# A third seven-product pair in two up panels, and both pairs in both wide down panels of the first part

## The chip, the cores and the metric

The kernel runs on one core of one Trainium2 chip. The metric is the device time of one execution in microseconds (us), the median over the timed runs. One further execution was recorded by the hardware profiler; every duration below comes from it unless it is called a run.

## What is computed

A decoder trunk of two layers over 256 tokens of width 2048, in float32. Layer 0 mixes tokens with gated linear attention, layer 1 with forgetting attention, and both cross-attend into 256 memory tokens. Behind each mixer stands the channel mixer, which is where the change lies:

```python
def causal_dwconv(u, w, b):
    up = jnp.pad(u, ((0, 0), (CONV_WIDTH - 1, 0), (0, 0)))
    return w[0] * up[:, 0:s_] + w[1] * up[:, 1:s_ + 1] + w[2] * up[:, 2:s_ + 2] + b

def conv_ffn(h, w_up, conv_w, conv_b, w_down):
    u = causal_dwconv(h @ w_up, conv_w, conv_b)
    a, val = split_cols(u, [FFN_HIDDEN, FFN_HIDDEN])
    return (jax.nn.silu(a) * val) @ w_down

for i in range(DEPTH):            # DEPTH = 2
    ...
    h = rmsnorm(x, norm_ffn[i])
    x = x + conv_ffn(h, ffn_w_up[i], ffn_conv_w[i], ffn_conv_b[i], ffn_w_down[i])
```

`w_up` is 2048 x 11264 and `w_down` 5632 x 2048, so the two mixers hold most of the matrix work.

## The kernel before, in words

**Numbers in two parts.** Every float32 operand x is split into hi (x rounded to the matmul format, a copy by ScalarE, ACT) and lo (x - hi, a subtraction by VectorE, DVE). One product is then three matmuls: hi by hi, lo by hi, hi by lo. Each weight is loaded raw from HBM in a unit of 128 x 1024 numbers (512 KB), cast by ACT (L257) and subtracted by DVE (L258) before TensorE (PE) can use it. Raw, hi and lo units lie in rings (`class Ring`, L193). In the channel mixer the hi and lo rings have five slots and one guest, and the raw ring five slots and three guests. A slot comes free when the matmuls that read it are done.

**Panels.** The channel mixer (`ffn`, L1419) is a list of panels. An up panel multiplies all 16 chunks of 128 inputs by 1024 columns of `w_up`; there are eleven per layer, and I call them up0 to up10 (`j` = 0, 4, ..., 40 in the code, so the sixth is up5 with `j` = 20 and the ninth up8 with `j` = 32). The hidden width is worked off in three parts (`PARTS`, of 16, 12 and 16 chunks). A wide down panel multiplies the chunks of a part by 1024 output columns. The first part has two of them, d0f0 and d0f2 (`f` = 0 and 2), the second d1f0 and d1f2. The order is up0 to up4, d0f0, d0f2, up5 to up7, d1f0, d1f2, up8 to up10, and then the last part. Every panel runs in each layer.

**Steps of a panel.** `pair_steps` (L409) works a panel off in places, one weight unit to a place. A single unit is a 2 x 2 block of products (two token blocks by two column halves), that is four products or 12 matmuls with 512 columns. Two neighbouring units k and k + 1 make a 2 x 2 by 2 x 2 block product with eight products; if sums of the activation blocks are at hand, they are done with seven (Winograd's form of Strassen's method), 21 matmuls instead of 24. Such a pair, which I call a seven, takes two places. It needs sums of the weight blocks too: four subtractions by DVE (L462 to L465), and four splits (L405 by ACT, L406 by DVE, one of 512 columns and three of 1024) where two singles need two. The dictionary `sums` says which units are paired, and `ahead` at which place.

**Accumulators.** A panel sums into eight accumulators, which are all the banks of PSUM. Seven-only ones (p1, p5, p7, p6) are written by sevens alone, the others (p2, p4, p3, x) by singles as well. After the last seven of a panel `early` (L1373 or L1526) reads the first four; after the last unit, always the single 15 (or 11), `late` (L1385, L1537) reads the other four. `flip` swaps the two sets of banks from panel to panel: the next panel's singles write first into the banks that `early` has read, and its sevens into those that `late` has read. All these reads are DVE instructions, beside one or two ACT copies. In a down panel `early` is eight DVE instructions, four of which add into x (L523).

**Activation sums.** `input_sums(k)` (L1471) makes the sums of the inputs h[k], h[k + 1] for the up panels: two additions of 128 x 256 (L1475), and in `token_sums` (L497) four of 128 x 128 (L501 to L504), a cast by ACT and a subtraction of 128 x 512 by DVE (L713). They are kept in `up_sums` for all panels of a layer: units 6, 7 for every up panel, and units 11, 12 for the panels in `MORE_IN`. For the down panels `gated` (L1458) makes the sums of the hidden chunks when these become known, in two rooms called dsum0 and dsum1; chunks 4, 5 and 10, 11 of the first part have them.

**Work between the steps.** What an up panel yields is scaled, transposed between the partitions by DVE and DMA, put through the convolution (`tap_of` on ACT, `add_tap` on DVE at L1450), silu and product, and split (`gated`, L553 and L554). It is emitted in small pieces between the steps of the following panels: `tick` (L1505) is called once for each place, and hands out pieces by a credit of 1.45 (1.7 beside the panels in `MORE_IN`); the two places of a seven get none. A panel's yield costs 20.4 of such credit. The yield of up4 is put off by 21 places (`PUT_OFF`), so that it falls into d0f2 and up5.

**Order on the engines.** The program is emitted step by step; a planner then fixes each engine's order from estimated times, and gives the weight splits an advance of 300 instructions (`high_priority`). On the chip each engine works its list off in that fixed order.

Of the kernel before, what the change touches and what calls it, by code (L numbers as in the profile page):

```python
# [34 lines left out]
SEVEN_UP = (6,)  # L35
SEVEN_DOWN = {4: 0, 10: 1, 20: 0, 34: 1}
SEVEN_MORE = 11
# [3 lines left out]
RAW_GUESTS = 3  # L41
PUT_OFF = {16: 21}
FIRST_DOWN = (10,)
UP_AHEAD = {8: 1, 40: 1}


LEVELS = (64, 16, 4)
# [105 lines left out]
def _trunk(ctx: ExitStack, tc: tile.TileContext, xt, xtok, memt, wp, wgu, gns, gfin, cnv, par, msk, out):  # L153
# [252 lines left out]
            lows.append(V.tensor_tensor(lo[:, :n], src, hi[:, :n].bitcast(F32), ALU.subtract))  # L406
        return hi, lo

    def pair_steps(units, src, sums, flip, pool, early, late, ahead=0):  # L409

        bank = {}
        fast, slow = ("p1", "p5", "p7", "p6"), ("p2", "p3", "p4", "x")
# [7 lines left out]
        plan = []  # L420
        at = 0
        while at < n:
            if at + ahead in sums:
                plan.append(at + ahead)
                at += 2
            else:
                plan.append(single.pop(0))
                at += 1
# [939 lines left out]
                    steps[f](u)  # L1368


    def down_pair(l, p, f, src, sums, flip, pool, temps, then=None):

        def early(bank):  # L1373
            t0, t1 = temps()
            S.activation(t0, bank["p1"], AF.Copy)
            add_to(f)(0, t0)
            V.tensor_tensor(t0, bank["p6"], t0, ALU.add)
            V.tensor_tensor(t1, bank["p7"], t0, ALU.add)
            add_to(f)(1, t1)
            add_to(f + 1)(1, t1)  # L1380
            add_to(f + 1)(1, bank["p5"])
            V.tensor_tensor(t0, bank["p5"], t0, ALU.add)
            add_to(f + 1)(0, t0)

        def late(b, h, a):  # L1385
            held_back = then is not None and h and not b and then.rooms is not None
            with tc.issue_after(then.turned[-1].ins) if held_back else nullcontext():
                add_to(f + h)(b, a)
            if then is not None:
                then(f + h, b)  # L1390

        return pair_steps(where["down", l, p, f], src, sums, flip, pool, early, late)

    def add_out(key, src, then=None, spare=None, last=None, first=0, hooks=None, late=1):

# [23 lines left out]
    def ffn(l, nx, h, m, more, ys, zs, landing, then, pool, temps, last=None, spare=None):  # L1419
        with tc.tile_pool(name=f"ffn{l}", bufs=1) as fp:  # L1420
            def held(name, i):
                return pool.tile([P, 2, 4, P], F32R, name=name, tag=f"{name}{i}")
# [48 lines left out]
            def input_sums(k):  # L1471

                r = temps(3).rearrange("p (s t) -> p s t", s=2)
                for s in range(2):
                    V.tensor_tensor(r[:, s, :], h[k + s][:, 0, :].bitcast(F32), h[k + s][:, 1, :].bitcast(F32), ALU.add)  # L1475
                token_sums(r, up_sums[k])
# [42 lines left out]
            def up_pair(j):  # L1519

                count[2] += 1
                second = j // 4 in MORE_IN
                turns = [turn(j + 2 * h_, PUT_OFF.get(j) or (7 if not h_ and j // 4 + 1 in MORE_IN else 8)) for h_ in range(2)]
                u = {}

                def early(bank):  # L1526
                    u.update({(b, h_): temps(2 * b + h_) for b in range(2) for h_ in range(2)})
                    S.activation(u[0, 1], bank["p1"], AF.Copy)
                    S.activation(u[0, 0], bank["p1"], AF.Copy, scale=scale(0))
                    V.tensor_tensor(u[0, 1], bank["p6"], u[0, 1], ALU.add)  # L1530
                    V.tensor_tensor(u[1, 0], bank["p7"], u[0, 1], ALU.add)
                    V.tensor_tensor(u[0, 1], bank["p5"], u[0, 1], ALU.add)
                    V.tensor_tensor(u[1, 1], bank["p5"], u[1, 0], ALU.add)
                    for b, h_ in ((0, 1), (1, 0), (1, 1)):
                        S.activation(u[b, h_], u[b, h_], AF.Copy, scale=scale(b))

                def late(b, h_, a):  # L1537
                    with tc.issue_after(turned_last[0].ins) if h_ and not b else nullcontext():
                        V.scalar_tensor_tensor(u[b, h_], a, scale(b), u[b, h_], ALU.mult, ALU.add)
                    turns[h_](b, u[b, h_])  # L1540

                return pair_steps(where["up", l, j], h, {k: up_sums[k] for k in (*SEVEN_UP, SEVEN_MORE)[: 1 + second]},
                                  count[2] % 2, pool, early, late, UP_AHEAD.get(j, 2 * second))

            def first(k):
                {2: lambda: nx.land(landing[0]), 3: nx.take, 8: nx.col,
# [5 lines left out]
            def drive(steps, share=1.45):  # L1552
                for k in steps:
                    tick(share if k >= 0 else 0.0)

            def drive_up(j):
                drive(up_pair(j), 1.7 if j // 4 in MORE_IN else 1.45)

            for k in SEVEN_UP:
                input_sums(k)  # L1560
# [3 lines left out]
            for p, (lo, hi) in enumerate(PARTS[:-1]):  # L1564
                while done < hi + 4:
                    drive_up(done)
                    done += 4
                src = [m[c % RING] for c in range(lo, hi)]
                for f in (0, 2):
                    count[2] += 1  # L1570
                    drive(down_pair(l, p, f, src, {c - lo: t for c, t in sums.items() if (c in FIRST_DOWN) == (f == 0)}, count[2] % 2, pool,
                                    lambda: (temps(0), temps(1))))
                sums.clear()
            lo, hi = PARTS[-1]
            while done < hi:
# [90 lines left out]
    with tc.tile_pool(name="stash", bufs=1) as st:  # L1666
# [4 lines left out]
        with tc.tile_pool(name="turn1", bufs=1) as tp:  # L1671
# [4 lines left out]
            def temps(i):  # L1676
                return fixed[i] if i < 2 else tp.tile([P, 512], F32, name="temp", tag=f"temp{i}")
# [149 lines left out]
```

## Time and profile before

| | |
|---|---|
| median of 3 runs | 2205.3 us (2204.51 to 2207.61) |
| the profiled execution, its own time | 2206.67 us |
| its span, first to last instruction | 2204.9 us |
| busy: POOL | 137.3 us (6%) |
| mean granted TensorE clock | 0.999 |

The span is the profiled execution without what lies around it (1.77 us). A busy share is an average over the whole span; the engines overlap. In a row of a group, the numbers are the engine's busy time, the mean duration of one instruction in ns, and the engine's idle time just before these instructions with what ended it. In a row of a timeline they are start and duration in us. In a row of windows they are the stretch, its length, each engine's busy time with its number of instructions, the granted clock, the DMA share and GB/s.

### The profile page before, as it was taken

The numbers are of one execution on the slowest core, as the hardware profiler recorded it, in microseconds if no ns is written. First come the engines' busy times: TensorE is split into PE (matmuls) and PEld (weight loads), VectorE is DVE, ScalarE is ACT, GpSimd is POOL, SyncE is SP. The second block draws the span as 40 slices with busy tenths as digits, with TensorE's granted clock in tenths as the row PEclk, the third lists the DMA queues.
The fourth block names the chain that finished last, engine by engine and source line by source line (L and its number), as shares of the span: only waits on it lengthen the run. The fifth ranks groups of instructions, "written<-read, shape, count | busy, mean of one in ns | idle before, by whom it ended". The sixth has DMA issues, their size and how long they took to land.

```text
span 2204.9 us, 30083 instructions
## 1 busy us (share of the span) xinstructions
PE 2192.4 (99%) x10285; PEld 1845.2 (84%) x10285; DVE 1836.0 (83%) x2731; ACT 1437.9 (65%) x2282; POOL 137.3 (6%) x257
## 2 busy tenths in 40 slices
PE   9999999999999999999999999999999999999998
PEld 7888888888888888888888998887888888888886
DVE  7768976679998889888987669668999888988996
ACT  6655655556785668657765555555878567765884
POOL 0000000001110010001010000000100001101100
PEclk9999999999999999999999999999999999999999
DMA  9767666777777677767777767676777657766773
GB/s 365 258 222 221 191 212 224 254 234 258 246 259 231 197 225 252 232 205 244 251 241 238 226 201 246 225 242 229 255 263 245 218 197 249 240 230 205 238 273 108
DMA packets 166289, 515.40 MB, mean 234 GB/s; under 512 B 20780, under 2 KB 42552, under 8 KB 166136
## 3 DMA queue, kind: packets, MB, share of 16 engines
q1 hardware_dynamic: 149064, 460.99, 63.4%
q0 software_dynamic: 16496, 51.71, 7.4%
q8 instruction: 80, 1.31, 0.2%
q10 hardware_dynamic: 576, 0.79, 0.1%
q14 instruction: 73, 0.60, 0.1%
HBM read 469.62 MB, written 43.79 MB: 233 GB/s over the span
## 4 chain that ended last, share of the span: by engine, by line
PE 98%; DMA 1%; DVE 0%; ACT 0%; SPq 0%; issue 0%; DVEq 0%; ACTq 0%
PE acc L435 30%; PE acc L362 26%; PE ps_s L435 15%; PE ps_o L435 8%; PE ps_t L435 7%; PE acc L288 3%; PE acc L333 3%; PE ps_s L362 2%; PE acc L392 2%; PE acc L286 1%; DMA raw<-wp 1%; PE ps_s L1060 0%; PE ps_o L726 0%; DMA far<-blk 0%; PE ps_s L726 0%; PE ps_s L1333 0%
## 5 line engine op out<-in xcount | busy, mean ns | idle before, releaser
L258 DVE TENSOR_TENSOR wlo<-raw,whi 128x1024 fp32r<-128x1024 f32 (+2 forms) x613 | 732.1, 1202 | 221.3 <-ACT whi L257 205.5
L257 ACT ACTIVATE whi<-raw 128x1024 fp32r<-128x1024 f32 (+2 forms) x613 | 636.6, 1044 | 368.0 <-PE acc L362 138.2
L362 PE MATMUL acc<-whi,B 128*128 128x512 f32 (+3 forms) x1248 | 290.8, 369 | 0.0
L362 PEld LDWEIGHTS acc<-whi,B 128*128 128x128 f32 x1248 | 226.8, 188 | 28.1
L405 ACT ACTIVATE whi<-raw 128x1024 fp32r<-128x1024 f32 (+1 forms) x154 | 146.6, 952 | 121.4 <-PE ps_t L435 32.5
L406 DVE TENSOR_TENSOR wlo<-raw,whi 128x1024 fp32r<-128x1024 f32 (+1 forms) x154 | 167.4, 1089 | 17.9 <-ACT whi L405 12.8
L435 PE MATMUL acc<-whi,mix 128*128 128x512 f32 x666 | 171.2, 389 | 1.5 <-ACT whi L257 1.5
L435 PE MATMUL acc<-whi,B 128*128 128x512 f32 x650 | 170.9, 389 | 0.0
L362 PE MATMUL acc<-wlo,B 128*128 128x512 f32 (+3 forms) x624 | 159.1, 369 | 0.0
L435 PEld LDWEIGHTS acc<-whi,mix 128*128 128x128 f32 x666 | 124.9, 188 | 27.8 <-ACT whi L257 1.9
L435 PEld LDWEIGHTS acc<-whi,B 128*128 128x128 f32 x650 | 122.0, 188 | 25.4
L1443 ACT ACTIVATE tap<-fvt,cw 128x256 f32<-128x256 f32 x264 | 123.9, 532 | 8.2 <-DMA fvt<-far 7.1
L1443 ACT ACTIVATE tap<-yzu,cw 128x256 f32<-128x256 f32 x264 | 123.8, 531 | 7.5 <-DMA yzu<-far 6.2
L362 PEld LDWEIGHTS acc<-wlo,B 128*128 128x128 f32 x624 | 114.2, 188 | 14.6
L1450 DVE TENSOR_TENSOR tap<-tap,tap 128x1024 f32<-128x1024 f32 x88 | 107.3, 1219 | 0.1
L435 PE MATMUL acc<-wlo,B 128*128 128x512 f32 x325 | 96.2, 389 | 0.0
L435 PE MATMUL acc<-wlo,mix 128*128 128x512 f32 x333 | 95.0, 389 | 0.0
L435 PE MATMUL ps_s<-whi,mix 128*128 128x512 f32 x332 | 92.6, 389 | 0.0
L435 PE MATMUL ps_s<-whi,B 128*128 128x512 f32 x282 | 79.3, 389 | 0.0
L435 PEld LDWEIGHTS acc<-wlo,mix 128*128 128x128 f32 x333 | 62.5, 188 | 13.0
L435 PEld LDWEIGHTS ps_s<-whi,mix 128*128 128x128 f32 x332 | 62.3, 188 | 12.9
L435 PEld LDWEIGHTS acc<-wlo,B 128*128 128x128 f32 x325 | 61.0, 188 | 12.7
(545 smaller groups left out, 4295.7 us busy)
## 6 DMA issues: line engine op xcount, KB each, us to landing
raw<-wp SPq DMA_DIRECT2D x741, 512.0 KB, 4.5
fvt<-far POOLq DMA_DIRECT2D x100, 128.0 KB, 4.8
raw<-wp SPq DMA_DIRECT2D x32, 384.0 KB, 3.6
far<-yu POOLq DMA_DIRECT2D x22, 512.0 KB, 3.4
far<-yzu POOLq DMA_DIRECT2D x22, 512.0 KB, 3.2
yzu<-far POOLq DMA_DIRECT2D x88, 128.0 KB, 4.7
raw<-wp SPq DMA_DIRECT2D x24, 388.0 KB, 3.6
x<-xtok SPq DMA_DIRECT2D x8, 512.0 KB, 7.6
```

The lines of the kernel that those rows point to most:

```text
L257: casts.append(S.activation(hi[:, s], raw[:, s], AF.Copy))
L258: lows.append(V.tensor_tensor(lo[:, s], raw[:, s], hi[:, s].bitcast(F32), ALU.subtract))
L286: mm = TE.matmul(acc[p][c][:, :T], w[:, s], both[:, 0, :], start=False, stop=end and j == 3)
L288: mm = TE.matmul(acc[p][c], w[:, s], both, start=u == j == 0, stop=end and j == 3)
L333: mm = TE.matmul(acc[b][:, :n], src[kcs[j] - base][:, part, b * P : (b + 1) * P], w, start=u == 0 and low == part == j == 0, stop=u == end ...
L362: mm = TE.matmul(acc[b][:, :n], src[kc - base][:, part, b * P : (b + 1) * P], ready[low][:, j * room : j * room + n], start=i == low == pa ...
L392: mm = TE.matmul(acc[b][:, :n], src[kc - base][:, part, b * P : (b + 1) * P], w, start=i == low == part == j == 0, stop=i == end and low = ...
L405: casts.append(S.activation(hi[:, :n], src, AF.Copy))
L406: lows.append(V.tensor_tensor(lo[:, :n], src, hi[:, :n].bitcast(F32), ALU.subtract))
L435: r = TE.matmul(bank[name], x, w, start=name not in begun, stop=last)
L1443: S.activation(by_run(taps[i][:, s, c, i:]), zs[slot][:, :, 2 * c + s], AF.Copy if i else AF.Identity, bias=0.0 if i else w[3], scale=w[2 ...
L1450: V.tensor_tensor(taps[0], taps[0], taps[n][:, :, :, :T], ALU.add)
```

## The change

Up panels get a table of places instead of `ahead`: the key is the place, the value the first unit of the pair.

```diff
-UP_AHEAD = {8: 1, 40: 1}
+UP_STEPS = ({6: 6}, {4: 6, 9: 11}, {1: 6, 5: 11, 10: 2}, {5: 6, 10: 11})
+THIRD, THIRD_IN = 2, (5, 8)
+LATER_IN = (2, 10)
...
-    def pair_steps(units, src, sums, flip, pool, early, late, ahead=0):
+    def pair_steps(units, src, sums, flip, pool, early, late, at_step):
...
-            if at + ahead in sums:
-                plan.append(at + ahead)
+            if at in at_step:
+                plan.append(at_step[at])
...
+                at_step = UP_STEPS[second + (j // 4 in THIRD_IN) + 2 * (j // 4 in LATER_IN)]
...
             def drive_up(j):
-                drive(up_pair(j), 1.7 if j // 4 in MORE_IN else 1.45)
+                share = 1.7 if j // 4 in MORE_IN else 1.45
+                if j // 4 == THIRD_IN[0]:
+                    up_sums[THIRD] = held("dsum", 1)
+                steps = up_pair(j)
+                if j // 4 == THIRD_IN[0]:
+                    for _ in range(4):
+                        tick(share if next(steps) >= 0 else 0.0)
+                    input_sums(THIRD)
+                drive(steps, share)
...
-                    drive(down_pair(l, p, f, src, {c - lo: t for c, t in sums.items() if (c in FIRST_DOWN) == (f == 0)}, count[2] % 2, pool,
-                                    lambda: (temps(0), temps(1))))
+                    steps = down_pair(l, p, f, src, {c - lo: t for c, t in sums.items() if not p or (c in FIRST_DOWN) == (f == 0)}, count[2] % 2, pool,
+                                      lambda: (temps(0), temps(1)), at_step=None if p else {5: 4, 10: 10})
+                    drive(steps)
```

Read out panel by panel: up0 to up4, up6, up7, up9 and up10 keep their pairs and places. up5 and up8 had pairs 6 and 11 at places 4 and 9; they get pair 6 at place 1, pair 11 at place 5 and a new pair 2 at place 10. d0f0 had pair 10 at place 10, and d0f2 pair 4 at place 4; both get pair 4 at place 5 and pair 10 at place 10. The sums for the new pair 2 are made once per layer, in up5 behind four places, in the room dsum1 that d0f2 has just read. The panels of the second and third part's down keep theirs.

More of the change, by code (lines that the diff above doesn't have):

```diff
@@ L1368, in fox, with down_pair @@
                     steps[f](u)
[L1371 removed]
+    def down_pair(l, p, f, src, sums, flip, pool, temps, then=None, at_step=None):
         def early(bank):
@@ L1390, in late @@
                 then(f + h, b)
-        return pair_steps(where["down", l, p, f], src, sums, flip, pool, early, late)
+        return pair_steps(where["down", l, p, f], src, sums, flip, pool, early, late, at_step or {k: k for k in sums})
     def add_out(key, src, then=None, spare=None, last=None, first=0, hooks=None, late=1):
@@ L1540, in late @@
                     turns[h_](b, u[b, h_])
-                return pair_steps(where["up", l, j], h, {k: up_sums[k] for k in (*SEVEN_UP, SEVEN_MORE)[: 1 + second]},
-                                  count[2] % 2, pool, early, late, UP_AHEAD.get(j, 2 * second))
+                at_step = UP_STEPS[second + (j // 4 in THIRD_IN) + 2 * (j // 4 in LATER_IN)]
+                return pair_steps(where["up", l, j], h, {k: up_sums[k] for k in at_step.values()}, count[2] % 2, pool, early, late, at_step)
             def first(k):
```

## The prediction

> **What bounds the kernel now.** I read the page first, from the busy shares to the chain that ended last.
>
> ```profile
> span 2204.9 us, 30083 instructions
> ...
> PE 2192.4 (99%) x10285; PEld 1845.2 (84%) x10285; DVE 1836.0 (83%) x2731; ACT 1437.9 (65%) x2282; POOL 137.3 (6%) x257
> ...
> PE 98%; DMA 1%; DVE 0%; ACT 0%; SPq 0%; issue 0%; DVEq 0%; ACTq 0%
> ...
> L257 ACT ACTIVATE whi<-raw 128x1024 fp32r<-128x1024 f32 (+2 forms) x613 | 636.6, 1044 | 368.0 <-PE acc L362 138.2
> L405 ACT ACTIVATE whi<-raw 128x1024 fp32r<-128x1024 f32 (+1 forms) x154 | 146.6, 952 | 121.4 <-PE ps_t L435 32.5
> L406 DVE TENSOR_TENSOR wlo<-raw,whi 128x1024 fp32r<-128x1024 f32 (+1 forms) x154 | 167.4, 1089 | 17.9 <-ACT whi L405 12.8
> L435 PE MATMUL acc<-whi,mix 128*128 128x512 f32 x666 | 171.2, 389 | 1.5 <-ACT whi L257 1.5
> L1450 DVE TENSOR_TENSOR tap<-tap,tap 128x1024 f32<-128x1024 f32 x88 | 107.3, 1219 | 0.1
> ```
>
> PE is busy 99% and carries 98% of the chain. The channel mixer's matmuls (L435) waited 1.5 us in this group, for an ACT cast. ACT, in contrast, waits for PE: the rings are full and the splits run as far ahead as the slots allow. So time goes where matmuls go, as long as DVE keeps up. Next I asked how full the panels are that the change touches, with the view of windows. The first three stretches are d0f0, d0f2 and up5 of layer 0, then up7, d1f2, up8; the last two are up5 and up8 of layer 1.
>
> ```profile
> core 0: us, PE busy (x) PEld busy (x) DVE busy (x) ACT busy (x) POOL busy (x), PEclk, DMA share, GB/s
> 669.26:712.11 42.85, 42.85 (x191) 35.48 (x190) 37.46 (x48) 22.01 (x28) 5.49 (x10) 1.00 0.74 239
> 712.11:754.94 42.83, 42.83 (x190) 35.47 (x189) 36.91 (x43) 30.28 (x47) 0.00 (x0) 1.00 0.61 203
> 754.94:797.10 42.16, 42.16 (x187) 34.91 (x186) 34.02 (x40) 22.87 (x25) 0.00 (x0) 1.00 0.61 199
> 839.26:881.42 42.16, 42.16 (x187) 34.91 (x186) 40.93 (x51) 35.62 (x57) 5.50 (x10) 1.00 0.73 238
> 914.06:946.02 31.96, 31.96 (x142) 26.46 (x141) 31.84 (x42) 19.61 (x28) 0.00 (x0) 1.00 0.69 224
> 946.02:988.18 42.16, 42.16 (x187) 34.91 (x186) 33.70 (x38) 22.87 (x25) 0.00 (x0) 1.00 0.62 204
> 1791.40:1833.56 42.16, 42.16 (x188) 34.91 (x187) 34.02 (x40) 22.85 (x25) 0.00 (x0) 1.00 0.60 199
> 1982.48:2024.64 42.16, 42.16 (x188) 34.91 (x187) 35.37 (x41) 22.75 (x25) 0.00 (x0) 1.00 0.64 216
> ```
>
> In every row PE is busy for the whole stretch. ACT has 12 us to spare where the change works, DVE 5 to 9. In up7 DVE is busy 40.93 of 42.16 us and in d1f2 31.84 of 31.96, and PE still has no gap. The clock is granted in full, so fewer matmuls are less time.
>
> **The matmuls that go.** A busy PE is not yet PE at its peak, so I take the spacing of starts.
>
> ```profile
> 1000.42 0.61 PE L435 MATMUL ps_s<-whi,usum 128*128 128x512 f32 x2
> 1000.88 0.39 PE L435 MATMUL ps_s<-wlo,usum 128*128 128x512 f32 x1
> 1001.10 0.61 PE L435 MATMUL acc<-whi,usum 128*128 128x512 f32 x2
> ```
>
> One product is three matmuls and the next begins 0.68 us later, 0.227 us each. up5 from these: 186 matmuls, 42.2 us, which is its window. A seven saves one product, 0.68 us. New sevens per layer: one each in d0f0, d0f2, up5, up8, which makes eight in two layers, 24 matmuls, 8 x 0.68 = 5.44 us. The Trainium skill (TensorE: Matmul & The Clock Gate, the part on 56 ns against 53.3 ns) has a warm matmul of 512 columns start every 215.7 ns; by it the saving would be 24 x 0.2157 = 5.2 us. The trace has 227 ns at full clock, and I use that.
>
> **What DVE and ACT get.** A seven has four splits in place of two, and four weight subtractions. Here is DVE around the border of d0f0 and d0f2 (712.11), with two of these kinds, and below it the parts of the input sums.
>
> ```profile
> 707.54 0.69 DVE L1382 TENSOR_TENSOR fvt<-acc,fvt 128x512 f32<-128x512 f32 x1
> 708.14 1.22 DVE L258 TENSOR_TENSOR wlo<-raw,whi 128x1024 fp32r<-128x1024 f32 x1
> 709.27 0.69 DVE L523 TENSOR_TENSOR x<-x,fvt 128x512 f32<-128x512 f32 x1
> 709.88 0.69 DVE L406 TENSOR_TENSOR wlo<-raw,whi 128x512 fp32r<-128x512 f32 x1
> 710.48 0.69 DVE L523 TENSOR_TENSOR x<-x,ps_o 128x512 f32<-128x512 f32 x1
> 711.08 0.68 DVE L523 TENSOR_TENSOR x<-x,ps_s 128x512 f32<-128x512 f32 x1
> 711.67 0.69 DVE L462 TENSOR_TENSOR raw<-raw 128x512 f32<-128x512 f32 x1
> ...
> L1475 DVE TENSOR_TENSOR temp<-B x4: 418/420/427, 466.1 to 507.3; 128x256 f32<-128x256 f32 x4
> L504 DVE TENSOR_TENSOR temp<-temp x4: 292/294/298, 467.8 to 1552.2; 128x128 f32<-128x128 f32 x4
> ```
>
> By durations a seven adds on DVE 4 x 1.09 + 4 x 0.69 - 2 x 1.22 = 4.7 us. But packed instructions start closer than they last: 0.60 us apart at 512 columns (710.48, 711.08, 711.67), 1.13 at 1024 (708.14 to 709.27). So it takes 0.60 + 3 x 1.13 + 4 x 0.60 - 2 x 1.13 = 4.1 us of DVE's time; that is the value I take, since DVE will be packed. The input sums of pair 2, once a layer in up5, are 2 x 0.42 + 4 x 0.29 + 0.69 = 2.7 us, about 2.1 packed. ACT gets 4 x 0.95 - 2 x 1.04 = 1.7 us a seven, which its 12 us take in.
>
> up8: 33.70 + 4.1 = 37.8 of 41.5 us, in layer 1 39.5. Both are below up7's 97%, so I price up8 at nothing.
>
> d0f0, d0f2 and up5 follow each other: idle DVE today is 5.39 + 5.92 + 8.14 = 19.45 us, of which 3 x 0.68 = 2.04 goes with the matmuls, leaving 17.4. The addition is 3 x 4.1 + 2.1 = 14.5 us packed (16.8 by durations). DVE ends at 123 of 125.8 us, 98%, like up7 and below d1f2. This is where the change can fail; while the splits keep any of their lead it costs nothing. That lead is at most the six slots of the hi and lo rings; a single unit is 12 x 0.227 = 2.72 us of PE, so it is five or six units, about 14 us, and half that where sevens use a slot every 0.68 to 1.36 us.
>
> Fewer ticks: d0f2 goes from 11 to 9 ticks behind the put-off of up4's yield, 13.05 of its 20.4 credits, so 7.35 instead of 4.45 spill into up5. There 10 ticks x 1.7 = 17 are at hand and nothing else waits. up8 has none waiting. Nothing is priced, and the cover is the spare credit.
>
> Wait on dsum1: the new sums need the room that d0f2's pair 10 reads; its matmuls end four singles before up5 begins, and the sums come two units later. Behind that ACT cast are weight casts with several units of lead. Zero. The weight loads, one queue, 512 KB a unit: 16 units in 41.5 us are 202 GB/s, and today's windows already carry 239. Zero.
>
> **Two edits whose cost the trace doesn't show.** These rows of DVE are from the end of d0f2 and the start of up5 (754.94) today.
>
> ```profile
> 739.91 0.69 DVE L1463 TENSOR_TENSOR tap<-tap 128x512 f32<-128x512 f32 x1
> ...
> 753.84 1.27 DVE L523 TENSOR_TENSOR x<-x,acc 128x512 f32<-128x512 f32 x2
> 755.03 0.42 DVE L554 TENSOR_TENSOR mix<-tap,mix 128x256 fp32r<-128x256 f32 x1
> ...
> 756.90 0.68 DVE L523 TENSOR_TENSOR x<-x,acc 128x512 f32<-128x512 f32 x1
> ```
>
> First, d0f2's `early` moves from behind place 5 to behind place 11, next to up4's yield. d0f0 has it there today: its last bank read ends at 708.2 (L1382), and d0f2 needs that bank at 712.11 + 0.45, a margin of 4.3 us. In d0f2 two tap additions (2 x 1.22) and one product with two splits (0.69 + 2 x 0.42) can get in between, 4.0 us: 0.3 would remain. Second, up5's first seven at place 1 writes the banks that `late` of d0f2 reads. Today they are wanted at place 4, 10.9 us in; then the first is wanted at 754.94 + 2.72 = 757.7 and the last five products later, at 761.1. `late` reads the first until about 754.5 and the last until 757.6: margins of 3.2 and 3.5 us. For both together: zero below, for PE has no gap there to win, and above, two weight splits that the planner lets ahead of such a read, 2.3 us a layer (a PE that has waited at the border for `early` finds `late` done). I take zero, because the state is nearest to d1f2, where DVE is 99.6% busy and PE without a gap.
>
> **Sum.** -5.44 us and nothing back: the profiled execution goes from 2206.67 to 2201.2, its span from 2204.9 to 2199.5; the profiled one is 1.4 us above the median, and from the median, 2205.3 - 5.44 = 2199.9 us.
>
> **Rivals.** *Full saving* (the forecast, 60%): 2199.9. For it speak the windows without a gap at 97 to 99.6% DVE.
>
> *A wait at the border of d0f2 and up5* (27%): one of the two margins is used up, since DVE has more queued there than in any panel now. Some 2 us per layer: 2199.9 + 4 = 2203.9, no change that can be told (about 0.2%, 4.4 us, is what a measurement of this kernel can tell from none). Against it: the margins of 3.2 and 4.3 us, and the planner may put these reads first.
>
> *DVE becomes the bound from d0f0 to up5* (8%): idle DVE is not free where a full ring causes it, because a split that waits for a slot blocks everything behind it on DVE. If only half of the 17.4 us can be filled, 8.7, then 14.5 - 8.7 = 5.8 us a layer come on PE once the lead is used: 2199.9 + 11.6 = 2211.5, slower. It turns the sign at 2.7 us a layer, and is slower by over 0.2% from 4.9, that is when under 9.6 us can be filled. Against it: d1f2 left only 0.12 us idle. The Trainium skill (VectorE: DVE Perf Modes, the parts on the DRAIN and on rules for kernel authors) has the next DVE instruction wait for the pipe to empty and advises few instructions; the change adds 62. By that rule the addition would be the 16.8 us, 0.6 short of all the idle time. The starts 0.60 us apart against durations of 0.69 disagree with it, and the measurement decides.
>
> *Something else* (5%): the planner's order shifts elsewhere by a microsecond or two either way; the one wait of 1.5 us in the first row of L435 could go or double.
>
> **How the numbers follow.** Faster by over 0.2% means below 2200.9: nearly all of the first case less what the spread of runs (2204.51 to 2207.61) takes at so thin a margin, 0.57. Within 0.2%: the border wait and that remainder, 0.34. Slower by over 0.2%: 0.09. The range runs from the full saving with the 1.5 us wait gone, 2198.4, to the border wait at 2203.9. The forecast's own range is 2199.1 (the lowest run less 5.44) to 2200.9.
>
> **What would show it.** PE at 10261 matmuls, DVE 2793 instructions, windows of d0f0, d0f2, up5, up8 at 42.16, 42.16, 41.48 and 41.48 us with PE busy throughout and DVE at 95 to 99%. A PE gap at the first singles or the first seven of up5, released by DVE reading p5 or x (L1382, L523), means the border wait. Gaps in up5's sevens released by L406 or L258 mean DVE is the bound. Windows still without gaps and a span that shrinks by less than 5 us would prove the accounting wrong.

## The result, and the profile after

The changed kernel takes 2229.45 us (median of 4 runs, 2227.1 to 2231.19), the kernel before beside it 2205.36 (2204.51 to 2207.61): a ratio of 1.0108 [1.0096, 1.0119]. It is slower by 24 us. The forecast was 2199.9, and the range ended at 2203.9. The profiled execution took 2230.87 us.

These are the lines of the page after that answer to those of before; the last one is a row of before that the prediction didn't show. The line numbers of the change are two higher (L435 is now L437, L258 is L260, L406 is L408), those of the taps too.

```profile
span 2229.1 us, 30023 instructions
...
PE 2198.5 (99%) x10261; PEld 1837.8 (82%) x10261; DVE 1865.0 (84%) x2793; ACT 1444.1 (65%) x2300; POOL 137.2 (6%) x257
...
PE 52%; DMA 4%; DVE 3%; ACT 2%; issue 1%; POOL 0%; SPq 0%; DVEq 0%; ACTq 0%; POOLq 0%
...
L437 PE MATMUL acc<-whi,mix 128*128 128x512 f32 x642 | 171.3, 389 | 1.0 <-ACT whi L259 1.0
L1445 ACT ACTIVATE tap<-fvt,cw 128x256 f32<-128x256 f32 x264 | 122.9, 531 | 21.4 <-DMA fvt<-far 16.7
...
L1443 ACT ACTIVATE tap<-fvt,cw 128x256 f32<-128x256 f32 x264 | 123.9, 532 | 8.2 <-DMA fvt<-far 7.1
```

The counts are the forecast ones: 24 matmuls fewer, 62 DVE instructions and 18 of ACT more. PE is still "busy 99%" (2198.5 of 2229.1 us): some 30 us of waits are little in such a span, and the whole-kernel share hides what happened. The chain tells it: PE carried 98% of it before. Now 52% is PE, and DMA, DVE and ACT have entered; not all of the chain is named in that line. Next the windows, of d0f0, d0f2, up5, then up6, up7, and d1f2, up8, all in layer 0 (the columns are those explained above: stretch, length, PE, weight load, DVE, ACT, POOL, clock, DMA).

```profile
669.58:711.74 42.16, 42.16 (x188) 34.92 (x186) 40.15 (x55) 24.62 (x33) 5.49 (x10) 1.00 0.64 229
711.74:753.90 42.16, 42.16 (x188) 34.92 (x186) 35.34 (x44) 25.22 (x39) 0.00 (x0) 1.00 0.53 185
753.90:801.05 47.15, 43.62 (x184) 33.65 (x183) 41.63 (x51) 25.77 (x32) 0.00 (x0) 1.00 0.53 179
801.05:846.34 45.29, 43.08 (x188) 34.60 (x186) 37.32 (x44) 31.22 (x50) 5.54 (x10) 1.00 0.76 230
846.34:890.19 43.85, 42.52 (x187) 34.77 (x186) 40.23 (x53) 32.49 (x49) 5.51 (x10) 1.00 0.66 241
922.83:956.16 33.33, 32.82 (x142) 26.20 (x141) 29.84 (x39) 22.83 (x37) 0.00 (x0) 1.00 0.51 169
956.16:999.88 43.72, 42.41 (x184) 34.04 (x183) 39.50 (x47) 24.54 (x29) 0.00 (x0) 1.00 0.60 209
```

d0f0 and d0f2 come out at 42.16 us, as forecast. up5 was to take 41.48 and takes 47.15. From here on I call *loss* of a panel its time from its first matmul to that of the next panel, less 0.227 us for each of its matmuls. In layer 0: up5 5.67, up6 3.13, up7 1.69, d1f2 1.37, up8 2.24, and the down panels of the last part 2.3 more than before; another 1.2 comes between them and up0 of layer 1. In layer 1: 4.60, 0.49, 1.73, 2.07, 2.74, and 0.5 in the last part. All panels ahead of up5 lose what they lost before or less. The two layers' losses add up to 29.7 us; less the 5.44 saved that is 24.3, and the spans differ by 24.2. So there are two questions: why up5 loses 10.3 us, and why panels that the change leaves alone, or that were right by themselves, lose some 19.

For the first question, here is the border of d0f2 and up5 (753.90), first on PE, then on DVE, in rows of the two timelines (start, duration, and in brackets the engine's idle time and what ended it).

```profile
746.87 0.62 PE L437 MATMUL ps_t<-whi,dsum 128*128 128x512 f32 x2
...
748.91 0.39 PE L437 MATMUL ps_t<-wlo,dsum 128*128 128x512 f32 x1
...
764.19 0.74 PE L437 MATMUL ps_s<-moremk,B 128*128 128x512 f32 x2 [0.38 <-ACT moremk L407]
...
769.98 0.50 PE L437 MATMUL acc<-moremv,usum 128*128 128x512 f32 x1 [0.40 <-DVE moremv L408]
...
787.20 1.19 PE L437 MATMUL acc<-moremk,dsum 128*128 128x512 f32 x4 [1.66 <-ACT moremk L407]
```

```profile
749.34 0.69 DVE L1379 TENSOR_TENSOR fvt<-ps_t,fvt 128x512 f32<-128x512 f32 x1 [2.12 <-PE ps_t L437]
...
768.10 0.68 DVE L525 TENSOR_TENSOR x<-x,acc 128x512 f32<-128x512 f32 x1
768.70 1.22 DVE L408 TENSOR_TENSOR moremv<-raw,moremk 128x1024 fp32r<-128x1024 f32 x1
```

The next row is the window around the border in the changed kernel; below it stands the same stretch of the kernel before, counted from its own border (754.94).

```profile
749.30:782.60 33.30, 31.43 (x132) 24.13 (x132) 33.16 (x43) 16.10 (x20) 0.00 (x0) 1.00 0.46 157
...
750.34:783.64 33.30, 33.30 (x149) 27.57 (x148) 26.54 (x31) 18.31 (x22) 0.00 (x0) 1.00 0.54 172
```

From 749.30 DVE works 33.16 of 33.30 us, against 26.54 before, and PE issues 132 matmuls where 147 fit. At 769.92 DVE ends a seven's split, and at 769.98 PE begins with it: no lead is left. One of `late`'s additions into x runs at 768.10, 14 us behind the border; before it ran at 756.90, 2 us behind it. And just ahead of this DVE stood for 2.12 us, because a product of d0f2's seven (the ps_t at 746.87 and 748.91) had been ordered among the matmuls of later singles, and `early` reads its bank.

These are all of PE's waits in up5 (engine and line, what ended the wait, us in total, times, longest).

```profile
PE acc L437 <- ACT moremk L407: 1.7, 1, 1.7
PE acc L437 <- DVE x L525: 0.5, 1, 0.5
PE acc L437 <- DVE moremv L408: 0.4, 1, 0.4
PE ps_o L437 <- DVE wlo L408: 0.4, 1, 0.4
PE ps_s L437 <- ACT moremk L407: 0.4, 1, 0.4
PE ps_o L437 <- ACT whi L259: 0.2, 1, 0.2
```

The prediction's two signs were a gap released by DVE's reads of a bank (the border wait) and one released by DVE's splits (DVE as the bound). Of these 3.5 us, 0.5 ends with an addition of `late`, 0.8 with splits of DVE, and the rest with casts of ACT, so neither sign is clean. The first of these casts had itself waited 0.8 us for a subtraction of DVE (L467). From start to start each wait costs some 0.3 us more than its idle time, which is how 3.5 us of waits make most of the 5.67: about 3.5 are lost by 772.7, beside the busy DVE, and 1.9 at 787.20, of which more below.

### The profile page after: what moved, and what is told of

The parts are those of the page before. It is cut to its first block, busy times and chain, and to the rows that moved or that the text cites. A ratio compares the mean times of both kernels' runs of the same rounds, so it can differ in the third digit from the quotient of the medians.

```text
span 2229.1 us, 30023 instructions
## 1 busy us (share of the span) xinstructions
PE 2198.5 (99%) x10261; PEld 1837.8 (82%) x10261; DVE 1865.0 (84%) x2793; ACT 1444.1 (65%) x2300; POOL 137.2 (6%) x257
## 4 chain that ended last, share of the span: by engine, by line
PE 52%; DMA 4%; DVE 3%; ACT 2%; issue 1%; POOL 0%; SPq 0%; DVEq 0%; ACTq 0%; POOLq 0%
PE acc L437 17%; PE acc L364 10%; PE ps_s L437 9%; PE ps_o L437 5%; PE ps_t L437 4%; PE acc L290 2%; PE acc L394 2%; PE acc L288 1%; DMA raw<-wp 1%; DMA yzu<-far 1%; PE acc L335 1%; PE ps_s L364 1%; DVE wlo L408 1%; DMA fvt<-far 1%; ACT tap L1445 1%
## 5 line engine op out<-in xcount | busy, mean ns | idle before, releaser
L259 ACT ACTIVATE whi<-raw 128x1024 fp32r<-128x1024 f32 (+2 forms) x601 | 621.2, 1043 | 394.3 <-PE acc L364 137.5
L260 DVE TENSOR_TENSOR wlo<-raw,whi 128x1024 fp32r<-128x1024 f32 (+2 forms) x601 | 713.9, 1199 | 171.2 <-ACT whi L259 152.8
L364 PEld LDWEIGHTS acc<-whi,B 128*128 128x128 f32 x1248 | 226.8, 188 | 28.1
L408 DVE TENSOR_TENSOR wlo<-raw,whi 128x1024 fp32r<-128x1024 f32 (+1 forms) x180 | 193.8, 1081 | 34.5 <-ACT whi L407 26.6
L407 ACT ACTIVATE whi<-raw 128x1024 fp32r<-128x1024 f32 (+1 forms) x180 | 169.2, 944 | 49.7 <-PE acc L437 19.0
L437 PE MATMUL acc<-whi,mix 128*128 128x512 f32 x642 | 171.3, 389 | 1.0 <-ACT whi L259 1.0
L437 PE MATMUL acc<-whi,B 128*128 128x512 f32 x608 | 164.1, 389 | 0.0
L437 PEld LDWEIGHTS acc<-whi,mix 128*128 128x128 f32 x642 | 120.2, 188 | 26.9 <-ACT whi L259 1.8
L1445 ACT ACTIVATE tap<-fvt,cw 128x256 f32<-128x256 f32 x264 | 122.9, 531 | 21.4 <-DMA fvt<-far 16.7
L1445 ACT ACTIVATE tap<-yzu,cw 128x256 f32<-128x256 f32 x264 | 122.9, 530 | 20.9 <-DMA yzu<-far 16.0
L437 PEld LDWEIGHTS acc<-whi,B 128*128 128x128 f32 x608 | 114.0, 188 | 24.0 <-ACT whi L259 0.4
L364 PEld LDWEIGHTS acc<-wlo,B 128*128 128x128 f32 x624 | 114.2, 188 | 14.6
L437 PE MATMUL acc<-wlo,mix 128*128 128x512 f32 x321 | 96.0, 389 | 0.0
L437 PE MATMUL ps_s<-whi,mix 128*128 128x512 f32 x316 | 92.9, 389 | 0.0
L437 PE MATMUL acc<-wlo,B 128*128 128x512 f32 x304 | 92.8, 389 | 0.0
L437 PE MATMUL ps_s<-whi,B 128*128 128x512 f32 x296 | 87.6, 389 | 0.0
L437 PEld LDWEIGHTS acc<-wlo,mix 128*128 128x128 f32 x321 | 60.3, 188 | 12.5
L437 PEld LDWEIGHTS ps_s<-whi,mix 128*128 128x128 f32 x316 | 59.3, 188 | 12.4
L364 PE MATMUL acc<-whi,mix 128*128 128x512 f32 x264 | 66.4, 391 | 1.9 <-ACT whi L259 1.9
```

The source lines that it names most:

```text
L259: casts.append(S.activation(hi[:, s], raw[:, s], AF.Copy))
L260: lows.append(V.tensor_tensor(lo[:, s], raw[:, s], hi[:, s].bitcast(F32), ALU.subtract))
L364: mm = TE.matmul(acc[b][:, :n], src[kc - base][:, part, b * P : (b + 1) * P], ready[low][:, j * room : j * room + n], start=i == low == pa ...
L407: casts.append(S.activation(hi[:, :n], src, AF.Copy))
L437: r = TE.matmul(bank[name], x, w, start=name not in begun, stop=last)
L1445: S.activation(by_run(taps[i][:, s, c, i:]), zs[slot][:, :, 2 * c + s], AF.Copy if i else AF.Identity, bias=0.0 if i else w[3], scale=w[2 ...
```

## The experiments

All times of a kernel are medians of runs, against the kernel before on the same chip (2205.2 to 2205.9 us on each); losses and waits are of the one profiled execution. Four theories went in. *A*: the planner, foreseeing late splits, strews a seven's products among others on PE, and the strewn order itself makes the loss. *B*: three sevens within one panel leave DVE too little time. *C*: too many sevens follow each other in d0f0, d0f2 and up5, however they are placed. *D*, which came up behind the first four runs: DVE's work is piled up at the border of d0f2 and up5, where three lists of it meet: the last seven and all of `early` of d0f2 (eight DVE instructions; five of them add into x, not four as said above), `late`, and the first seven of up5 at place 1.

**Each half alone: `down_only`, `up_only`.**

```diff
 # down_only
-THIRD, THIRD_IN = 2, (5, 8)
+THIRD, THIRD_IN = 2, (99, 99)
 # up_only
-{... if not p or (c in FIRST_DOWN) == (f == 0)}, ..., at_step=None if p else {5: 4, 10: 10})
+{... if (c in FIRST_DOWN) == (f == 0)}, ..., at_step=None)
```

> Only d0f0 and d0f2 take both pairs; up5 and up8 keep two pairs at places 4 and 9. Matmuls alone would give 2205.4 - 4 x 0.68 = 2202.7 us. Theory A (the planner's order: with more VectorE work in its estimate it strews the matmuls of a seven among those of later units, so weight slots and banks come free late and a cast blocks ScalarE's queue): d0f2 is already strewn in the changed kernel, so part of the loss is here, some 8 to 15 us, 2211 to 2218. Theory B (VectorE has too little time in three sevens within up5 and up8): nothing is lost here, 2202.7. Theory C (VectorE has too little time over d0f0, d0f2 and up5 together): a third of the load is gone, no loss, about 2203.

> Only up5 and up8 take the third pair; d0f0 and d0f2 keep one pair each. Matmuls alone would give 2205.4 - 4 x 0.68 = 2202.7 us. Theory A (the planner's order): the loss of up8 and d1f2 stays, 2 x 3 to 4 us, and that of up5 in part: 2208 to 2215. Theory B (too little VectorE time within three sevens of one panel): nearly the whole loss of 27 to 29 us is here, 2225 or more. Theory C (too little over d0f0, d0f2 and up5 together): up5 alone fits, 2203.

`down_only` took 2207.99 us against 2205.88 (1.001 [1.0001, 1.002]): the 2.7 us are saved, and up6 loses 1.97 and 2.63. None of the theories had that: A said 2211 or more, B and C about 2203. `up_only` took 2202.49 (0.9985 [0.9976, 0.9994]): faster by 3.4 us, and no panel loses anything; that is C's 2203, and A and B fail. The matmuls are 2.7 us of it; in the profiled execution up0 of layer 1, which lost 1.8 us before, loses nothing here. Its up5, with three sevens, places 1, 5 and 10, and a busy DVE:

```profile
711.97:754.81 42.84, 42.84 (x191) 35.47 (x189) 37.26 (x45) 28.94 (x44) 0.00 (x0) 1.00 0.50 160
754.81:796.29 41.48, 41.48 (x185) 34.35 (x183) 38.04 (x45) 25.21 (x30) 0.00 (x0) 1.00 0.73 240
```

The halves sum to -1.3 us, both together are +24. So neither half is the fault, and a third seven at place 1 of up5 is none by itself: what d0f2 leaves behind must meet it.

**PE in the program's order: `after_pinned`, `before_pinned`.** Each matmul of the wide panels is issued after the one before it in the program.

```diff
-            r = TE.matmul(bank[name], x, w, start=name not in begun, stop=last)
+            with tc.issue_after(in_order[-1].ins) if in_order else nullcontext():
+                r = TE.matmul(bank[name], x, w, start=name not in begun, stop=last)
+            in_order[:] = [r]
```

> The changed kernel, with each matmul of the channel mixer's wide panels put behind the one before it in the order of the program, so that the planner cannot mix units; VectorE's and ScalarE's work is the same. Theory A (the planner's order of PE): the loss goes, 2200 to 2206. Theories B and C (VectorE has too little time, in one panel or in three): the same loss, 2225 or more, since the work is all there.

> The kernel before with the same pinning, as a measure of what pinning itself does. Theory A: PE had next to no gap before, so at most a few us either way, 2203 to 2209. Theories B and C say nothing different of this one: 2203 to 2209.

`after_pinned` took 2253.18 us (1.0209 [1.0193, 1.0225]), `before_pinned` 2227.69 (1.0103 [1.0086, 1.012]), where 2203 to 2209 was expected: the planner's mixing is worth 22 us to the old kernel too. With the order held the change still costs 25.5. Held to its order, up5 loses 8.93 us in either layer, where the pinned kernel before loses nothing, and in layer 0 all of PE's waiting there is one wait for a split of DVE:

```profile
PE acc L439 <- DVE wlo L409: 6.3, 1, 6.3
```

So A falls as the cause of the first loss. The 25.5 are not the changed kernel's loss over again, though: the two d0f0 lose 9.5 us in `after_pinned` and nothing in the changed kernel, and of the 8.93 some 2.3 us are a halved clock behind the wait (last section). Also, d1f2 and up8 lost nothing there, and they do lose in the changed kernel; I come back to it with `pinned_late`.

**One down panel at a time: `d0f0_alone`, `d0f2_alone`.** The other one keeps its one seven at its old place.

```diff
-if not p or (c in FIRST_DOWN) == (f == 0)}, ... at_step=None if p else {5: 4, 10: 10})
+if not p and not f or (c in FIRST_DOWN) == (f == 0)}, ... at_step=None if p or f else {5: 4, 10: 10})      # d0f0_alone
+if not p and f or (c in FIRST_DOWN) == (f == 0)}, ... at_step=None if p or not f else {5: 4, 10: 10})      # d0f2_alone
```

> The changed kernel, but d0f2 keeps its one pair at place 4; d0f0 has both pairs, up5 and up8 three. Matmuls alone: 2205.9 - 6 x 0.68 = 2201.8 us. Theory D (a stack at one border: d0f2's late pair, its bank reads behind it, up4's put-off work, and up5's sevens at places 1 and 5 want more VectorE time within some 25 us than the lead covers): the stack is taken apart, no loss, 2201 to 2204. Theory C (VectorE has too little time over d0f0, d0f2 and up5 together): two thirds of the excess stay, a loss of 8 us or more, 2210 or more.

> The changed kernel, but d0f0 keeps its one pair at place 10; d0f2 has both pairs at 5 and 10, up5 and up8 three. Matmuls alone: 2201.8 us. Theory D (a stack at the border of d0f2 and up5): the stack is whole, so the loss of the changed kernel stays nearly whole, 2220 to 2230. Theory C (three panels together): as much relief as without d0f2's second pair, so the same time as that kernel, within 3 us.

`d0f0_alone` took 2203.78 us (0.9992 [0.9983, 1.0002]), up5 losing 0.94 and 0.91: as D has it. `d0f2_alone` took 2211.18 (1.0025 [1.0016, 1.0034]), up5 losing 1.77 and 1.69 and up7 3.47 in layer 0. That is slower, and yet 9 us short of what D expected, and C's number was missed as well. Both panels add to the loss: d0f0's second seven costs a little by itself, and much more where d0f2's late one follows it.

**The same sevens, sooner: `d0f2_early`, `eight_spaced`, `eight_spaced_2`.** Eight new sevens as in the change, with only the places in d0f2, or in d0f0 and d0f2, moved.

```diff
-at_step=None if p else {5: 4, 10: 10})
+at_step=None if p else {1: 4, 5: 10} if f else {5: 4, 10: 10})      # d0f2_early
+at_step=None if p else {1: 4, 5: 10} if f else {3: 4, 7: 10})       # eight_spaced
+at_step=None if p else {2: 4, 6: 10} if f else {3: 4, 7: 10})       # eight_spaced_2
```

> The changed kernel with the same eight new sevens, but d0f2's pairs at places 1 and 5 in place of 5 and 10, so that its bank reads end well before up5 and before most of up4's put-off work. Matmuls alone: 2200.5 us. Theory D (stack at the border): most of the loss goes, 2200 to 2208. Theory C: VectorE's work over the three panels is the same, so the loss stays, 2225 or more; the sevens of d0f2 come sooner behind those of d0f0, which could open a new gap in d0f2.

> All eight new sevens, as in the changed kernel, but d0f0's pairs at places 3 and 7 and d0f2's at 1 and 5 (up5 at 1, 5 and 10 as changed). Matmuls alone 2200.0 us. Theory D (it is the place, and VectorE's time next to it, that costs): less than the 6 us that the same sevens lost with d0f0 at 5 and 10, 2200 to 2206. Theory C (the amount over three panels costs, wherever it stands): as d0f2_early, 2205 or more.

> As eight_spaced, but d0f2's pairs at places 2 and 6. Theory D: d0f2's bank reads come one place later, closer to up5, a little more loss than eight_spaced or the same, 2200 to 2207. Theory C: the same as eight_spaced within 1 us, 2205 or more.

`d0f2_early` took 2205.25 us (0.9999 [0.999, 1.0009]), `eight_spaced` 2204.79 (0.9998 [0.9989, 1.0007]), `eight_spaced_2` 2205.78 (1.0001 [0.9992, 1.0011]). None of the three can be told from the kernel before. D's ranges hold all of them. C fails by 20 us in `d0f2_early`; the other two come within 0.2 us of C's numbers as well and don't part the theories. So moving two sevens of d0f2 gives back 24 us, with the same matmuls and the same splits. Here are d0f2 and up5 of `d0f2_early`, and the same 33.3 us at the border:

```profile
711.21:753.37 42.16, 42.16 (x188) 34.91 (x186) 39.12 (x46) 30.29 (x49) 0.00 (x0) 1.00 0.59 200
753.37:796.48 43.11, 42.62 (x184) 34.02 (x183) 39.46 (x48) 25.72 (x31) 0.00 (x0) 1.00 0.58 206
```

```profile
749.30:782.60 33.30, 32.81 (x141) 25.92 (x140) 30.69 (x38) 15.61 (x19) 0.00 (x0) 1.00 0.49 168
```

DVE is busy 39.12 us in d0f2, against 35.34 in the changed kernel, and the border is lighter for it. Still up5 loses 1.6 us a layer, and up6, up8 and up10 2.8 together over both layers; no spacing that I tried saves all eight: `eight_spaced` loses 4.2 us in all. In `eight_spaced_2`, with both places of d0f2 one later, up5 loses 5.41 and 2.37. In layer 0 that is nearly what it loses in the changed kernel (1.6 us of it are a halved clock, see the last section), and yet no panel behind it loses anything. So a late up5 doesn't have to bring the aftermath.

**The third pair in up8 alone: `third_in_up8`.** up5 keeps two sevens, at places 4 and 9.

```diff
-THIRD, THIRD_IN = 2, (5, 8)
+THIRD, THIRD_IN = 2, (8, 8)
```

> The changed kernel, but up5 keeps two pairs at places 4 and 9; d0f0 and d0f2 have both, up8 three. Matmuls alone: 2201.8 us. Theory D with an aftermath (what up7, d1f2 and up8 lose in the changed kernel comes from the disorder that the border left): d0f0 and d0f2 lose as without any third pair, some 4.6 us in up6, and up8 and d1f2 nothing: 2205 to 2208. If up8's third pair is too much by itself behind a loaded stretch, d1f2 and up8 lose their 3.6 to 4.8 us per layer again: 2214 or more.

It took 2211.73 us (1.0027 [1.0017, 1.0038]), 4 us above the expected range. up5 loses nothing, as expected, but up6 3.01 and 2.01, and up8 1.64 and 1.49. So the place-1 seven of up5 isn't needed for a loss: with two sevens each in d0f0 and d0f2 it shows later, in up6, as in `down_only`.

**Less work for DVE at the border: `less_vector`.** The changed kernel without the four weight subtractions of d0f2's seven at units 10, 11 and of up5's first seven, 16 instructions over two layers.

```diff
+                  if light == k:
+                    summed = lows[-1]
+                  else:
...
-        return pair_steps(..., at_step or {k: k for k in sums})
+        return pair_steps(..., at_step or {k: k for k in sums}, 10 if (p, f) == (0, 2) else None)
-                return pair_steps(..., at_step)
+                return pair_steps(..., at_step, 6 if j == 20 else None)
```

> The changed kernel without the four weight subtractions of d0f2's pair 10 and of up5's pair 6 (part of the computation is left out: these two sevens use unsummed weights); everything else, the matmuls, splits, banks and slots, is the same. That takes 8 x 0.60 = 4.8 us a layer off VectorE right at the border. Theory D in terms of VectorE's time: up5's loss of 4.6 to 5.7 us goes to under 1, and with it most of what the later panels lose: 2202 to 2210. If banks or weight slots are what is short at the border and not VectorE's time: 2222 or more.

```profile
span 2198.6 us, 30064 instructions
...
PE 2187.2 (99%) x10261; PEld 1840.1 (84%) x10261; DVE 1859.5 (85%) x2777; ACT 1443.4 (66%) x2300; POOL 136.9 (6%) x257
...
PE 98%; DMA 1%; DVE 1%; ACT 0%; issue 0%; SPq 0%; DVEq 0%; ACTq 0%
```

```profile
749.30:782.60 33.30, 33.08 (x147) 27.08 (x146) 28.77 (x34) 17.82 (x22) 0.00 (x0) 1.00 0.44 143
```

It took 2201.05 us (0.998 [0.9971, 0.999]). Sixteen instructions of 512 columns, 9.6 us at the spacing of 0.60, give back 28 us. At the border PE has its 147 matmuls and DVE is busy 28.77 us. From d0f0 on the only loss left is 0.79 in up5 of layer 0; up6, up7, d1f2, up8 and the last part lose nothing more than before. (1.8 us of the profiled execution's gain is another thing: up0 of layer 1 lost that much before, 1.5 in the changed kernel, and nothing here.) This shows that in the changed kernel the whole aftermath is set off at the border, and by DVE's steps there. It does not part DVE's time from the length of the chain subtract, cast, split, since the edit shortens both; `d0f2_early`, where the chains are as they were, speaks for the time. In both kernels the planner also orders the engines anew, and what that alone does was not measured.

**The aftermath: `pinned_late`, `taps_later`.** `pinned_late` is the changed kernel with PE held to the program's order from up6 to up8 alone; `taps_later` puts the yield of up5 off by 11 places besides.

```diff
+            with tc.issue_after(in_order[-1].ins) if in_order and pinned[0] else nullcontext():
 # in drive_up, behind drive(steps, share)
+                pinned[0] = 20 <= j < 32
 # taps_later
-PUT_OFF = {16: 21}
+PUT_OFF = {16: 21, 20: 11}
```

> The changed kernel with PE's matmuls kept in the order of the program from up6 to up8 alone; the border is left as it is. Theory E1 (what up6, up7, d1f2 and up8 lose, 15 us in both layers, comes from the strewn order that the planner gives PE there): these lose 3 us or less together, 2214 to 2219. Theory E2 (it comes from casts that stand in ScalarE's queue behind taps whose data is late): the same loss, 2225 to 2232.

> The kernel pinned_late, with up5's yield taken up 11 places after it instead of 7 and 8, so that its data has landed when ScalarE comes to the taps. Theory E2 (of what up6 and up7 lose in pinned_late, 9.7 us in both layers, the part behind taps that wait for data): up6's loss falls from 2.3 to 3.4 us to about 1.6, and the wait of 4.7 us goes; but the yield now runs into up7, so that up7 may lose more. 2216 to 2222 in all. If the taps' wait costs nothing, up6 loses as before.

`pinned_late` took 2220.77 us (1.007 [1.0055, 1.0085]), 8.7 under the changed kernel and between the ranges of E1 and E2. up5 loses what it lost (5.74 and 5.07), up6 3.35 and 2.31 and up7 2.03 twice; d1f2, up8 and the last part lose nothing. So the later part of the aftermath goes with the order on PE that the planner made behind up5. (Why it made it is in its estimates, which no trace shows.) That order is not all of it, since up8 loses again in `taps_later`, where PE is held in the same way. The earlier part has another face. These rows of the changed kernel are ACT in up5, and the waits that DVE and ACT had in up6 (engine and line, what ended the wait, us in total, times, longest).

```profile
776.67 1.05 ACT L407 ACTIVATE whi<-raw 128x1024 fp32r<-128x1024 f32 x1
784.19 2.00 ACT L259 ACTIVATE whi<-raw 128x1024 fp32r<-128x1024 f32 x2 [6.47 <-PE ps_s L437]
786.11 1.04 ACT L407 ACTIVATE moremk<-raw 128x1024 fp32r<-128x1024 f32 x1
```

```profile
ACT tap L1445 <- DMA fvt<-far: 8.3, 1, 8.3
...
DVE wlo L408 <- ACT whi L407: 7.9, 2, 5.5
```

ACT stands for 6.47 us on the cast of a single, whose slot PE has not yet freed, and behind it in the list waits the cast of the seven that PE wants next: it ends at 787.15, and PE, 1.66 us idle, goes on at 787.20. In up6 ACT stands for 8.3 us on a tap whose data comes late by DMA, with weight casts behind it, and DVE waits for those. On the page the wait for this DMA grew from 7.1 to 16.7 us (L1443 before, L1445 after). In `pinned_late` the tap's wait in up6 is still 4.7 us. `taps_later` was to take it away, and does: up6 loses 1.77 and 1.81 in place of 3.35 and 2.31. But it took 2227.22 us (1.0099 [1.0084, 1.0114]), 5 above its range; up5 lost 7.92 and 5.03, up7 2.16 and 3.75, and up8 2.80 and 2.69 again. The 2.2 us more in up5 of layer 0 are a longer wait there (2.40 us where `pinned_late` has 1.73) and a halved clock behind it, and lie ahead of the taps that were moved. So the late tap is part of up6's loss. The rest of it is, in both runs and both layers, mainly one wait of 1.5 us for a bank that `late` of up5 reads on DVE, and in up7 one of 1.7 to 1.8 us for a seven's split; up7 loses 1.0 a layer in `before_pinned` too, so part of that comes with holding the order. Why DVE is late there stays open, and so does why `down_only` loses two us a layer in up6, where PE waits 1.1 and 0.6 us for DVE's splits of singles and 0.3 and 0.8 for their casts.

**Fewer sevens: `d0f0_old_d0f2_early`, `d0f0_both_d0f2_early`.** The first adds six sevens over two layers in place of eight (d0f0 as before, d0f2 at places 1 and 5); the second gives d0f0 both and leaves d0f2 its one, at place 1 in place of 4.

```diff
-if not p or (c in FIRST_DOWN) == (f == 0)}, ... at_step=None if p else {5: 4, 10: 10})
+if not p and f or (c in FIRST_DOWN) == (f == 0)}, ... at_step=None if p or not f else {1: 4, 5: 10})      # d0f0_old_d0f2_early
+if not p and not f or (c in FIRST_DOWN) == (f == 0)}, ... at_step=None if p else {1: 4} if f else {5: 4, 10: 10})      # d0f0_both_d0f2_early
```

> d0f0 keeps its one pair at place 10, d0f2 takes both at places 1 and 5, up5 and up8 three: six new sevens, matmuls alone 2205.3 - 4.1 = 2201.2 us. Theory D: d0f0's second pair gone and d0f2's reads early leave no stack, a loss of at most 1 us: 2201 to 2202.5. Theory C (all of VectorE's work counts, wherever it stands): as d0f2_alone, some 6 us lost, 2207 or more.

> As d0f0_alone (d0f0 both pairs at 5 and 10, d0f2 pair 4, up5 and up8 three), but d0f2's pair stands at place 1 in place of 4: six new sevens, 2201.2 us by the matmuls. Theory D: d0f0_alone lost 1.85 us in the two up5; with d0f2's bank reads three places sooner that goes to under 1: 2201 to 2202.5. Theory C: the same as d0f0_alone, 2203.8.

The first took 2202.68 us (0.9987 [0.9978, 0.9996]), no panel losing anything more than before. The second took 2204.58 (0.9996 [0.9986, 1.0005]), losing 1.2 a layer in d0f2. That is outside D's 2201 to 2202.5 and nearer to C's 2203.8; up5 loses nothing there, as D has it, but a new loss has come up in d0f2. With `up_only` at 2202.49 that makes two versions that beat both kernels, by some 3 us, and there is no telling them apart.

## Why the prediction was wrong, point by point

**The matmuls that go: right.** The counts on the page are those forecast, d0f0 and d0f2 are 42.16 us, and in `up_only` up5 is 41.48. One matmul is 0.227 us of PE, and the 24 are 5.44 us; they are in every account of loss above.

**DVE: the step that failed.** It said that the addition fits into the idle time of d0f0, d0f2 and up5 together, and that "while the splits keep any of their lead it costs nothing". up5 lost 10.3 us over both layers, and 19 more came behind it. The prediction's own sign shows it: DVE was to be busy 95 to 99% of these panels, and in d0f2 it was 84% (35.34 of 42.16 us) while up5 lost 5.67. It was not that the addition is larger than priced. DVE's busy time on the page grew by 29.0 us, and my prices come to 2 x (4 x 4.1 + 2.1) = 37.0. The error was to sum idle time over 126 us, as if work could be shifted freely within them. In d0f2, where DVE had to work ahead, it could not: these are the waits of ACT and DVE in d0f2 of the changed kernel.

```profile
ACT moremk L407 <- PE acc L437: 8.1, 1, 8.1
ACT whi L259 <- PE acc L437: 7.8, 3, 4.7
DVE moremv L408 <- ACT moremk L407: 3.2, 1, 3.2
DVE fvt L1379 <- PE ps_t L437: 2.1, 1, 2.1
```

The casts wait for PE to free their slots, and DVE waits for the casts; 6.8 us of DVE passed idle in d0f2, and the next 33 us had none to spare. The comparison with d1f2 and up7, at 97 to 99.6%, misled me: up7 has two sevens and d1f2 one, and d1f2 shows that DVE can be full, not that more work at its border would go unnoticed.

**The weight loads at nothing: right for PE.** None of PE's waits in up5 ends with a load. ACT waits for one once, 3.7 us.

**The two moved edits: wrong.** I priced `early` of d0f2 behind place 11 and the seven at place 1 of up5 at zero, and at most 2.3 us a layer, "because the state is nearest to d1f2". up5 lost 5.67 and 4.60. The margin of 0.3 us that I had worked out for `early` was the warning. It was worked out from today's order, in which a seven's products stand together; in the changed kernel four of the seven stand among singles, and `early` read its bank at 749.34. `d0f2_early`, which takes this edit back, gave 24 us back; `up_only`, with the seven at place 1 alone, lost nothing. So it is the meeting of the two.

**The rivals.** "DVE becomes the bound from d0f0 to up5" was the right mechanism, with its reason: "a split that waits for a slot blocks everything behind it on DVE". It got 8% and 2211.5, since it priced what PE waits in those three panels and stopped there: 5.8 us a layer against the 5.1 measured. That the size agrees is luck, since the half of 17.4 us was a guess that no row bore out. The border wait (27%, 2203.9) shows in 0.5 us of PE's waits in up5, and is far too small. What no case had is the aftermath, 19 us behind up5, in which fixed lists on ACT and PE, as far as the runs show it, carry one lateness on for four panels and more.

The Trainium skill (TensorE: Matmul & The Clock Gate, Part 1, the paragraph on engine queue depths) calls the queues of ACT and DVE strictly first in, first out. The 6.47 us of ACT ahead of 784.19, with the needed cast behind it, agree with it.

**up8 at nothing: right by itself.** It loses nothing in `up_only`, in `less_vector` and in `pinned_late`. In the changed kernel it loses 2.24 and 2.74 as aftermath, and in `third_in_up8` 1.6 and in `taps_later` 2.7 to 2.8 a layer, which I have not explained.

## What to carry to other kernels

Idle time of an engine counts as room only in the stretch where the new work falls due, and only if nothing holds the engine up there: where its work waits for buffers that the bottleneck frees, it cannot be done ahead. So draw up the addition by tens of microseconds around each border, with everything that meets there, and not by three panels. And where each engine works off a fixed list, price a stall with what stands behind it: here 10 us at the border became 30, though in `eight_spaced_2` 7.8 us in up5 stayed 7.8.

## What the runs showed of the hardware

`after_pinned` shows the clock that a stall costs besides. PE stood idle for 6.3 us in up5; the rows are that wait, what followed, and the later part of up5.

```profile
768.90:775.19 6.29, 0.02 (x1) 0.00 (x1) 6.29 (x8) 1.54 (x2) 0.00 (x0) 0.86 0.26 83
775.19:780.40 5.21, 5.21 (x13) 4.11 (x14) 4.80 (x6) 1.97 (x2) 0.00 (x0) 0.51 0.77 278
780.40:790.00 9.60, 9.60 (x44) 7.94 (x43) 7.24 (x9) 5.94 (x9) 0.00 (x0) 1.00 0.74 223
```

For 5.2 us the granted clock was 0.51, and 13 matmuls took the time of 23. The Trainium skill (TensorE: Matmul & The Clock Gate, Part 1) has the clock halve after an idle window of some 3.4 us and come back after a busy one of that length; half a clock agrees, and so does its spacing of 426.7 ns when cold (two matmuls from 775.78 to 776.64 in this trace). The 5.2 us at half clock are longer than that. The same trace shows half clock after a wait of only 2.4 us, 0.50 from 695.50 to 698.10, and so do `taps_later` behind its wait of 2.40 us in up5 (first row) and `eight_spaced_2` behind two waits of 0.74 and 0.81 us there (second row), far below those 3.4 us:

```profile
787.60:791.40 3.80, 3.80 (x11) 2.97 (x11) 3.80 (x4) 3.80 (x6) 0.00 (x0) 0.55 0.89 288
...
787.40:790.80 3.40, 3.40 (x10) 2.70 (x9) 2.76 (x4) 2.17 (x3) 0.00 (x0) 0.51 0.78 276
```

In the changed kernel, whose largest single gap in up5 is 1.66 us, the clock stayed at 1.00 in every window of it shown above, so the clock has no part in its losses of up5 to up8.
